# The down product of two feed-forward networks by Strassen's scheme, with sums on VectorE and GpSimd

## The chip, the core and the metric

The kernel runs on one NeuronCore of a Trainium2 chip. Its engines are TensorE (PE, matrix products; its weight loads are shown as PEld), VectorE (DVE), ScalarE (ACT), GpSimd (POOL) and SyncE (SP, which issues most DMAs here). Each engine executes its own instructions strictly in the order in which the program lists them; between engines, semaphores make one wait for another. Matrix products accumulate in PSUM, everything else works on tiles in SBUF, and DMAs move data between DRAM and SBUF. The metric is the time on the device of one launch, in microseconds (us). Three runs of the kernel before took 3050.97 to 3052.87 us, median 3051.56.

## The reference

The model is one layer of a hybrid decoder over 16 meta tokens and 1024 tokens, with 1024 features: a half-step SwiGLU network, a middle part (chunked gated DeltaNet beside RWKV-7, merged and projected), a second half-step SwiGLU network, and a final RMS norm. The meta tokens are dropped from the output. The change touches the two networks, each of which adds half of this to the hidden state:

```python
def _swiglu(x, w_gu, w_down):
    gate, up = jnp.split(x @ w_gu, 2, axis=-1)
    return (jax.nn.silu(gate) * up) @ w_down
```

`w_gu` has 1024 x 5632 elements, `w_down` 2816 x 1024. All inputs are float32.

## The kernel before

Features lie on the 128 partitions and tokens run along a row, so a row block is 128 features by all tokens: 8 row blocks for the hidden state `h` (in the second network `hh`), 22 for the 2816 hidden features. The first network (`ffn1`, L647) has 1040 tokens, the second (`ffn2`, L729) 1024.

A float32 product is made of three TensorE products: each operand is split into a high and a low part (`split`, L155: ScalarE copies the high part, VectorE subtracts to get the low one), and high x high, high x low and low x high are summed in PSUM.

Weights come through `fetchw` (L216). In the order of a generator, it loads a raw tile `wraw` (two buffers) on SyncE's queue and splits it into a tile `w` (two buffers). `loadw` takes the next tile and has the one after it fetched. A raw buffer is free again when VectorE has read it, and a `w` buffer when TensorE has used it.

`gate_up` (L435) makes the two input products by a scheme of Strassen's kind, with 7 products instead of 8 of half blocks; in it GpSimd makes sums of weights (L418 to L421). It multiplies gate and up on VectorE (L538) and stores each hidden row block half by half to the DRAM tensor `hid` (`store`, L477). `Hidden` (L561) loads those rows again, whole, into `hr` (three buffers, 520 or 512 KB each) and splits them into `hd`. The first three loads are issued before `gate_up` ends.

`down` (L606) is the plain product. The 22 hidden rows come in groups of 6, 6, 5 and 5 (`GROUPS`). For each group and each of 8 output blocks m there is one weight tile, 768 or 640 columns wide, that serves two token chunks (528 + 512 tokens in the first network, 512 + 512 in the second; `halves` cuts 528 into 256 and 272). A product `pd` of a group and a chunk accumulates in PSUM, and VectorE adds half of it to `h` (L624). In the last group the chunks run one after the other, so that its weight tiles are loaded twice, and after each block a hook does the norm that follows: in `ffn1` the sums of squares and the scaled input of the middle part, in `ffn2` the final norm and the output. `h` is loaded again for this stage, on GpSimd's queue (L687, L770). `Rms` (L265) squares on ScalarE, adds on VectorE (L281), and sums over the partitions by a TensorE product with ones (L292).

The whole order of each engine is fixed when the program is built.

## Time and profile before

The profile is of one execution, whose span, from its first to its last instruction, is 3046.4 us; the median of the runs is 5.2 us longer, for what lies around the span.

| what | value |
|---|---|
| runs | 3050.97, 3051.56, 3052.87 us |
| span of the profiled execution | 3046.4 us |
| TensorE, VectorE, ScalarE, GpSimd busy | 97%, 66%, 45%, 11% of the span |
| mean granted clock of TensorE | 0.993 |
| matmuls of `down` (`pd`) | 2448 + 192, from 473.3 to 3031.1 us |
| weight tiles of `down` loaded | 48 of 320 KB, 32 of 384 KB |
| hidden loads `hr` | 22 of 520 KB, 22 of 512 KB |

"Busy" counts an instruction from its start to its end; matmuls overlap, so the duration of one matmul is not the time it takes up in a sequence. A row of a timeline gives the start, the duration, the engine, the line, the operation, what it writes and reads, and in brackets how long the engine was idle before and which instruction it waited for. A row of windows gives, for a stretch, each engine's busy time with its number of instructions, then the granted clock, the mean busy share of the 16 DMA engines and the GB/s that they moved.

### The profile page before, as it was taken

How to read it: one execution, taken by the hardware profiler on the slowest of the kernel's cores; microseconds unless marked ns; L12 is line 12 of the kernel's file. 1: busy time of each engine (PE TensorE's matmuls, PEld its weight loads, DVE VectorE, ACT ScalarE, POOL GpSimd, SP SyncE). 2: the span in 40 equal slices, each digit the busy share in tenths (PEclk: the TensorE clock that was granted, in tenths of full speed). 3: DMA queues.
4: the chain of work that ended last, by engine and by line, in shares of the span. 5: the costliest groups of instructions: out<-in, count | busy, mean ns of one | idle time of the engine just before them, and what ended most of it. 6: DMA issues, size and time to landing. Idle time of an engine off the chain costs nothing.

```text
span 3046.4 us, 61663 instructions
## 1 busy us (share of the span) xinstructions
PE 2942.3 (97%) x25498; PEld 2530.1 (83%) x25498; DVE 2007.7 (66%) x3872; ACT 1372.2 (45%) x2404; POOL 348.6 (11%) x503
## 2 busy tenths in 40 slices
PE   8999999999989999999998999999999999999998
PEld 8999998998878888888776777777786888888886
DVE  7555554346668877778868888777766755556246
ACT  5322222125645656556565655665544432223114
POOL 0322220000000000000000110010000032232000
PEclk9999999999999999999999999999999999999999
DMA  3232224234222322233332333223345132225223
GB/s 127 83 98 84 83 82 160 81 94 149 80 67 72 78 74 67 78 82 97 82 92 67 91 80 81 74 74 88 106 145 178 64 104 90 83 83 202 58 80 115
DMA packets 257593, 287.19 MB, mean 94 GB/s; under 512 B 169296, under 2 KB 175440, under 8 KB 257312
## 3 DMA queue, kind: packets, MB, share of 16 engines
q1 hardware_dynamic: 253072, 271.43, 30.2%
q0 software_dynamic: 2512, 8.65, 0.8%
q8 instruction: 201, 3.29, 0.5%
q10 hardware_dynamic: 1728, 3.16, 0.3%
q14 instruction: 80, 0.66, 0.1%
HBM read 232.70 MB, written 50.47 MB: 93 GB/s over the span
## 4 chain that ended last, share of the span: by engine, by line
PE 52%; DVE 10%; ACT 5%; issue 2%; DMA 1%; SPq 0%; DVEq 0%; ACTq 0%
PE pp L261 16%; PE pg L448 13%; PE pd L261 8%; PE pwo L261 3%; PE pg L472 1%; DVE w L160 1%; DVE tb L1400 1%; DVE Xb L1402 1%; ACT w L159 1%; PE vp L1085 1%; PE cs L1032 1%; PE mp L1085 1%; PE np L1085 1%; DVE mt L1508 1%; PE bkt L1317 1%
## 5 line engine op out<-in xcount | busy, mean ns | idle before, releaser
L261 PE MATMUL pp<-uk,w 128*128 128x512 f32 (+2 forms) x4824 | 966.6, 346 | 9.3 <-DVE w L160 5.7
L261 PEld LDWEIGHTS pp<-uk,w 128*128 128x128 f32 x4824 | 741.3, 190 | 105.5 <-DVE w L160 13.2
L159 ACT ACTIVATE w<-wraw 128x1024 fp32r<-128x1024 f32 (+2 forms) x330 | 326.4, 989 | 497.5 <-PE pd L261 301.7
L261 PE MATMUL pd<-hd,w 128*128 128x512 f32 (+2 forms) x2448 | 454.4, 346 | 5.3 <-ACT hd L159 3.1
L160 DVE TENSOR_TENSOR w<-wraw,w 128x1024 fp32r<-128x1024 f32 (+2 forms) x330 | 403.2, 1222 | 74.8 <-ACT w L159 64.9
L261 PEld LDWEIGHTS pd<-hd,w 128*128 128x128 f32 x2448 | 391.8, 189 | 63.9 <-ACT hd L159 3.3
L448 PE MATMUL pg<-bt,w 128*128 128x256 f32 (+2 forms) x2520 | 400.7, 317 | 0.0
L448 PEld LDWEIGHTS pg<-bt,w 128*128 128x128 f32 x2520 | 360.4, 188 | 32.8
L454 DVE TENSOR_TENSOR c<-c,pg 128x520 f32<-128x520 f32 (+1 forms) x280 | 189.6, 689 | 278.3 <-PE pg L448 250.6
L448 PE MATMUL pg<-b,w 128*128 128x256 f32 (+2 forms) x2160 | 347.8, 317 | 0.0
L448 PEld LDWEIGHTS pg<-b,w 128*128 128x128 f32 x2160 | 309.8, 188 | 28.0
L159 ACT ACTIVATE w<-wrx 128x1024 fp32r<-128x1024 f32 (+1 forms) x64 | 58.4, 913 | 289.8 <-PE pg L448 247.9
L418 POOL TENSOR_TENSOR wrx<-wrx 128x512 f32<-128x512 f32 x38 | 52.5, 1382 | 732.8 <-DVE w22b L160 519.0
L1402 DVE TENSOR_TENSOR Xb<-Xb,tb 115x126 f32<-115x126 f32 (+22 forms) x496 | 125.4, 253 | 9.1 <-DVE tb L1400 0.4
L1400 DVE TENSOR_TENSOR tb<-Ub,Xb 115x126 f32<-115x126 f32 (+22 forms) x496 | 124.1, 250 | 8.1 <-DMA Ub<-scr 0.9
L1209 DVE SCALAR_TENSOR_TENSOR acc<-xr,pk,acc 128x528 f32<-128x528 f32 (+1 forms) x144 | 108.8, 756 | 28.6 <-ACT acc L1205 28.0
L624 DVE SCALAR_TENSOR_TENSOR h<-pd,h 128x528 f32<-128x528 f32 (+1 forms) x64 | 44.6, 698 | 116.4 <-PE pd L261 116.4
L624 DVE SCALAR_TENSOR_TENSOR hh<-pd,hh 128x512 f32<-128x512 f32 x64 | 44.1, 690 | 115.2 <-PE pd L261 115.2
L261 PE MATMUL pwo<-uk,w 128*128 128x512 f32 x384 | 99.7, 413 | 4.1 <-DVE w L160 1.9
L261 PEld LDWEIGHTS pwo<-uk,w 128*128 128x128 f32 x384 | 73.8, 197 | 21.9 <-ACT w L159 2.7
L160 DVE TENSOR_TENSOR w<-wrx,w 128x1024 fp32r<-128x1024 f32 (+1 forms) x64 | 66.6, 1041 | 14.9 <-ACT w L159 14.8
L159 ACT ACTIVATE hd<-hr 128x1040 fp32r<-128x1040 f32 (+1 forms) x40 | 41.2, 1061 | 63.3 <-DMA hr<-hid 38.3
(420 smaller groups left out, 4200.4 us busy)
## 6 DMA issues: line engine op xcount, KB each, us to landing
wraw<-in_win SPq DMA_DIRECT2D x150, 512.0 KB
wraw<-in_wgu SPq DMA_DIRECT2D x44, 512.0 KB
wrx<-in_wgu SPq DMA_DIRECT2D x44, 512.0 KB
wraw<-in_wdn SPq DMA_DIRECT2D x48, 320.0 KB
wraw<-in_wdn SPq DMA_DIRECT2D x32, 384.0 KB
hid<-c SPq DMA_DIRECT2D x44, 260.0 KB
hr<-hid SPq DMA_DIRECT2D x22, 520.0 KB
hid<-c SPq DMA_DIRECT2D x44, 256.0 KB
```

The costliest lines, as they stand in the source:

```text
L159: g.nc.scalar.activation(hi, src, AF.Copy)
L160: (eng or g.nc.vector).tensor_tensor(lo, src, hi.bitcast(F32), op=ALU.subtract)
L261: g.nc.tensor.matmul(ps, lhsT=l, rhs=r, start=i == 0, stop=i == n - 1)
L418: sums.tensor_tensor(a22, a21, a22, op=ALU.add)
L448: nc.tensor.matmul(ps[:, c0 : c0 + cn], lhsT=l[:, x, k, :], rhs=r[:, k, y, c0 : c0 + cn], start=i == 0, stop=i == 3 * HK - 1)
L454: nc.vector.tensor_tensor(o, x, y, op=ALU.add)
L472: nc.tensor.matmul(ps[:, c0 : c0 + cn], lhsT=l[:, x, k, :], rhs=r[:, k, y, c0 : c0 + cn], start=i == 0, stop=i == 6 * HK - 1)
L624: nc.vector.scalar_tensor_tensor(hv, pd, 0.5, hv, op0=ALU.mult, op1=ALU.add)
L1085: g.nc.tensor.matmul(ps[e][HS[dst], c0 : c0 + CB], lhsT=l, rhs=r, start=True, stop=True)
L1209: nc.vector.scalar_tensor_tensor(acc[:, :n], xr[:, tap : tap + n], V("convw", ct * 4 + tap), acc[:, :n], op0=ALU.mult, op1=ALU.add)
L1400: nc.vector.tensor_tensor(tv, U[:, i, i + 1 :].unsqueeze(2).to_broadcast([npt, nt, ncc]), X[:, i, 0:ncc].unsqueeze(1).to_broadcast([npt, n ...
L1402: nc.vector.tensor_tensor(X[:, i + 1 :, 0:ncc], X[:, i + 1 :, 0:ncc], tv, op=ALU.add)
```

## The change

The product becomes one of 2 x 2 blocks: output rows 0 to 511 and 512 to 1023, hidden rows 0 to 1407 and 1408 to 2815, and two halves of the tokens (520 or 512 each). Winograd's form of Strassen's scheme needs 7 products of half blocks where the plain product has 8. For each of them the hidden side is a *form*, in the order `b11`, `t1`, `t2`, `b22`, `t3`, `b21`, `t4`: three blocks of the hidden rows and four differences. `gate_up` makes the differences with four more subtractions on VectorE for each pair of row blocks, and stores 7 x 11 rows of one half's width to `frm`.

The weight side is a block as it is (forms 0, 5, 6) or a sum or difference of blocks (forms 1 to 4), made by GpSimd in a resident tile `wsum`, each from the one before and one raw tile; forms 1 and 4 also load a second block straight into `wsum`. `down` then runs rounds over the forms and, in each, over four output blocks m with two weight tiles, of 6 and 5 row blocks of hidden features. Each product is added, halved, to up to four blocks of `h` (`ADDS`: 4, 2, 3, 1, 2, 1, 1). Hidden tiles have 28 slots and three buffers `hr` of half the former size.

In the first network the last two rounds run twice, first for columns 256 to 519, then for 0 to 255 (`by_columns`), so that the norm after them begins before all is done; the second sum of squares there is added by GpSimd. In the second network the final norm of one half of the tokens is made after round 4, that of the other at the end.

```diff
+CHUNKS = ((0, 6), (6, 5))
+
+FORMS = ("b11", "t1", "t2", "b22", "t3", "b21", "t4")
+ADDS = ((0, 1, 2, 3), (1, 3), (1, 2, 3), (1,), (2, 3), (0,), (2,))
+NSLOT = 28
+LAST = len(FORMS) - 2
...
+def down_rounds(by_columns):
+
+    for r in range(LAST):
+        yield r, None
+    for cols in ((256, T // 2 - 256), (0, 256)) if by_columns else (None,):
+        for r in range(LAST, len(FORMS)):
+            yield r, cols
...
-        f = 0
-        for G in GROUPS:
-            for _ in range(2 if f + G == NF else 1):
-                for m in range(KD):
-                    yield f"wdn{n}", (m, slice(None), slice(f, f + G)), G
-            f += G
+        for r, _ in down_rounds(n == 1):
+            for m in range(HK):
+                for k0, kk in CHUNKS:
+                    yield f"wdn{n}", (r, m, k0), kk
...
+def down_weights(g, name, raw, r, m, k0, kk):
+
+    blk = lambda i, j: g.a[name][m + HK * i][:, HF * j + k0 : HF * j + k0 + kk]
+    dma = g.nc.sync.dma_start
+    sums = g.nc.gpsimd.tensor_tensor
+    dma(raw, blk(*((0, 0), (1, 1), (0, 0), (0, 1), (1, 0), (0, 1), (1, 1))[r]))
+    if r in (0, LAST, LAST + 1):
+        return raw
+    s = g.wsum[:, m, k0 : k0 + kk]
+    if r == 1:
+        dma(s, blk(1, 0))
+        sums(s, s, raw, op=ALU.add)
+    elif r == 2:
+        sums(s, s, raw, op=ALU.subtract)
+    elif r == 3:
+        sums(s, raw, s, op=ALU.subtract)
+    else:
+        dma(s, blk(0, 0))
+        sums(s, s, raw, op=ALU.subtract)
+    return s
...
-    raw = g.wp.tile([P, KD, P], F32, name="wraw", tag="wraw", bufs=2)
-    g.nc.sync.dma_start(raw[:, :kk, :], g.a[name][idx])
+    raw = g.wp.tile([P, KD, P], F32, name="wraw", tag="wraw", bufs=2)[:, :kk]
+    if name.startswith("wdn"):
+        src = down_weights(g, name, raw, *idx, kk)
+    else:
+        src = raw
+        g.nc.sync.dma_start(raw, g.a[name][idx])
     w = g.wp.tile([P, 2, KD, P], F32R, name="w", tag="w", bufs=WB)
-    split(g, raw[:, :kk, :], w[:, 0, :kk, :], w[:, 1, :kk, :])
+    split(g, src, w[:, 0, :kk, :], w[:, 1, :kk, :])
...
+    def sub(o, x, y, p, form):
+        nc.vector.tensor_tensor(o, x, y, op=ALU.subtract)
+        store(o, p, form)
...
+            mul(c12, g12, p)
+            sub(g11, c12, c11, p, "t1")
+            sub(g22, c22, g11, p, "t2")
+            sub(c12, c22, c12, p, "t3")
...
+            mul(c21, g21, p, "b21")
+            sub(g21, c21, g22, p, "t4")
...
+    def fill(self, upto):
+        while len(self.at) < min(upto, len(self.order)):
+            rp = self.order[len(self.at)]
+            if not self.raws:
+                self.load()
+            t = self.slots.pop(0)
+            split(self.g, self.raws.pop(0), t[:, 0, :], t[:, 1, :])
+            self.at[rp] = t
...
-def down(g, sp, hs, which, chunks, hooks, hidden, bufs):
+def down(g, hs, which, n, hidden, hooks):
...
-    f0 = 0
-    for G in GROUPS:
-        hid = hidden.tiles(sp, f0, G, bufs)
-        last = f0 + G == NF
-        if last:
-            hooks.before_last()
-        for ci, cs in enumerate([[c] for c in chunks] if last else [chunks]):
-            for m in range(KD):
-                wd = loadw(g, f"wdn{which}", m, slice(None), slice(f0, f0 + G))
-                for t0, n in cs:
-                    pd = mm_tile(g, "pd", n)
-                    for c0, cn in halves(n):
-                        sl = slice(t0 + c0, t0 + c0 + cn)
-                        mm3(g, pd[:, c0 : c0 + cn], wd, G, lambda k: (hid[k][:, 0, sl], hid[k][:, 1, sl]))
-                    hv = hs[m][:, t0 : t0 + n]
-                    nc.vector.scalar_tensor_tensor(hv, pd, 0.5, hv, op0=ALU.mult, op1=ALU.add)
-                if last:
-                    hooks.after_block(ci, m)
-        f0 += G
+    hidden.fill(HF + 5)
+    for r, cols in down_rounds(which == 1):
+        hidden.fill(HF * (r + 1))
+        for m in range(HK):
+            pd = mm_tile(g, "pd", n)
+            parts = [cols] if cols else halves(n)
+            for k0, kk in CHUNKS:
+                wd = loadw(g, f"wdn{which}", r, m, k0)
+                for c0, cn in parts:
+                    for k in range(k0, k0 + kk):
+                        x = hidden.at[r, k]
+                        for i, (u, v) in enumerate(((0, 0), (0, 1), (1, 0))):
+                            nc.tensor.matmul(pd[:, c0 : c0 + cn], lhsT=wd[:, u, k - k0, :], rhs=x[:, v, c0 : c0 + cn],
+                                             start=k + i == 0, stop=k == HF - 1 and i == 2)
+            c0, cn = cols or (0, n)
+            for o in ADDS[r]:
+                t0 = o % 2 * n + c0
+                hv = hs[m + o // 2 * HK][:, t0 : t0 + cn]
+                nc.vector.scalar_tensor_tensor(hv, pd[:, c0 : c0 + cn], 0.5, hv, op0=ALU.mult, op1=ALU.add)
+            hooks.after(r, cols, m)
+            if r <= LAST:
+                hidden.fill(HF * r + 16 + 3 * (m + 1))
...
+        pairs = [k + i * HK for k in range(HK) for i in range(2)]
+        for k in pairs:
             nc.gpsimd.dma_start(hs[k], g.a["hT"][k])
+        sum_tile = lambda shape, dtype: sp.tile(shape, dtype, name="wsum", tag="wsum", bufs=1)
+        g.wsum = sum_tile([P, HK, HF, P], F32)
+        keep = [slot_tile(sp, n, f"fa{i}") for i in range(17)]
+        early = ExitStack()
+        ep = early.enter_context(tc.tile_pool(name="f1e", bufs=1, reuse_waits="tile"))
+        ring = keep[2:] + [slot_tile(ep, n, f"fb{i}") for i in range(NSLOT - 17)] + keep[:2]
+        hidden.slots = (2 * ring)[: LAST * HF] + keep[1:]
...
-            hooks.rms = [Rms(g, lambda: g.un.tile([P, 528], F32, name="nsq", tag="nsq", bufs=4), n)
-                         for _, n, _ in SEGS]
+            hooks.rms = [Rms(g, lambda: g.un.tile([P, 528], F32, name="nsq", tag="nsq", bufs=4), n,
+                             add_on=nc.gpsimd if s else None) for s, (_, n, _) in enumerate(SEGS)]
...
+            if r < LAST:
+                if r == LAST - 1 and m == HK - 1:
+                    before_last()
+                return
+            s = 0 if cols[0] else 1
...
+        def final_tiles(s):
+            new = lambda tag, m: sp.tile([P, m, n], F32, name="fin", tag=tag, bufs=1)
+            ts = [new("wsum", 11)] if s else [new(f"fs{i}", 2) for i in unused]
+            rows = [t[:, i, :] for t in ts for i in range(t.shape[1])]
+            hooks.rs, hooks.rows = rows[3], rows[4:]
+            it = iter(range(100))
+            return Rms(g, lambda: rows[next(it) % 3], n)
+
+        def after(r, cols, m):
+            s, k = int(r < LAST), m + HK * (r - LAST)
+            blk = lambda k: hs[k][:, s * n : (s + 1) * n]
+            if k < 0 and k + 1:
+                return
+            if s or k == 0:
+                hooks.sum = final_tiles(s)
+            for i in range(KD - 1) if s else [k] * (k < KD - 1):
+                hooks.sum.add(blk(i))
+            if not s and k < KD - 1:
+                return
+            rs = hooks.rs
+            hooks.sum.finish(rs, blk(KD - 1))
```

On VectorE, where the first network passes from `gate_up` to `down`. The rows of before: `hd` are splits of hidden rows, `w` splits of weight tiles, `h` the sums; the last row of `gate_up` stands first.

```order
L538 TENSOR_TENSOR c21_4826<-c21_4826,c21_4677 128x520
L160 TENSOR_TENSOR hd_4970<-hr_4639,hd_4970 128x1040
L160 TENSOR_TENSOR hd_4973<-hr_4641,hd_4973 128x1040
L160 TENSOR_TENSOR hd_4978<-hr_4976,hd_4978 128x1040
L160 TENSOR_TENSOR hd_4983<-hr_4981,hd_4983 128x1040
L160 TENSOR_TENSOR hd_4988<-hr_4986,hd_4988 128x1040
L160 TENSOR_TENSOR hd_5492<-hr_5490,hd_5492 128x1040
L624 SCALAR_TENSOR_TENSOR h0_4953<-pd_4991,h0_4953 128x528
L624 SCALAR_TENSOR_TENSOR h0_4953<-pd_5029,h0_4953 128x512
L160 TENSOR_TENSOR w_5051<-wraw_5049,w_5051 128x768
```

The same place of the change, from the fourth hidden split on (`fa` are slots for hidden tiles):

```order
L165 TENSOR_TENSOR fa5_5052<-hr_5084,fa5_5052 128x520
L165 TENSOR_TENSOR fa6_5053<-hr_5088,fa6_5053 128x520
L165 TENSOR_TENSOR fa7_5054<-hr_5092,fa7_5054 128x520
L165 TENSOR_TENSOR fa8_5055<-hr_5096,fa8_5055 128x520
L165 TENSOR_TENSOR fa9_5056<-hr_5100,fa9_5056 128x520
L165 TENSOR_TENSOR w_5175<-wraw_5173,w_5175 128x768
L165 TENSOR_TENSOR fa10_5057<-hr_5104,fa10_5057 128x520
L165 TENSOR_TENSOR fa11_5058<-hr_5108,fa11_5058 128x520
L165 TENSOR_TENSOR fa12_5059<-hr_5112,fa12_5059 128x520
L165 TENSOR_TENSOR fa13_5060<-hr_5116,fa13_5060 128x520
L673 SCALAR_TENSOR_TENSOR h0_5033<-pd_5136,h0_5033 128x520
L673 SCALAR_TENSOR_TENSOR h0_5033<-pd_5136,h0_5033 128x520
```

Where six whole hidden rows were split ahead of the first sum, there are twelve halves and a weight tile now, and more hidden splits follow between the sums.

On VectorE in the middle of a group before (only sums and weight tiles):

```order
L160 TENSOR_TENSOR w_5240<-wraw_5238,w_5240 128x768
L624 SCALAR_TENSOR_TENSOR h4_4957<-pd_5243,h4_4957 128x528
L624 SCALAR_TENSOR_TENSOR h4_4957<-pd_5281,h4_4957 128x512
L160 TENSOR_TENSOR w_5303<-wraw_5301,w_5303 128x768
L624 SCALAR_TENSOR_TENSOR h5_4958<-pd_5306,h5_4958 128x528
```

In round 1 of the change, for one output block m; behind it GpSimd's sums of the same round:

```order
L165 TENSOR_TENSOR w_5644<-wsum_5046,w_5644 128x768
L165 TENSOR_TENSOR fa8_5055<-hr_5778,fa8_5055 128x520
L165 TENSOR_TENSOR fa9_5056<-hr_5782,fa9_5056 128x520
L165 TENSOR_TENSOR fa10_5057<-hr_5868,fa10_5057 128x520
L673 SCALAR_TENSOR_TENSOR h1_5035<-pd_5596,h1_5035 128x520
L673 SCALAR_TENSOR_TENSOR h5_5036<-pd_5596,h5_5036 128x520
L165 TENSOR_TENSOR w_5696<-wsum_5046,w_5696 128x640
L165 TENSOR_TENSOR fa11_5058<-hr_5872,fa11_5058 128x520
L165 TENSOR_TENSOR fa12_5059<-hr_5876,fa12_5059 128x520
```

```order
L239 TENSOR_TENSOR wsum_5046<-wsum_5046,wraw_5549 128x768
L239 TENSOR_TENSOR wsum_5046<-wsum_5046,wraw_5597 128x640
L239 TENSOR_TENSOR wsum_5046<-wsum_5046,wraw_5640 128x768
L239 TENSOR_TENSOR wsum_5046<-wsum_5046,wraw_5692 128x640
L239 TENSOR_TENSOR wsum_5046<-wsum_5046,wraw_5735 128x768
```

Each step has two weight splits that read `wsum`, with two or three hidden splits of the next round among them, and GpSimd has two sums for it, where it had none in this stage.

On TensorE before, in the first group of the first network, where one weight tile passes from the first chunk to the second:

```order
L261 MATMUL pd_5306<-hd_4983,w_5240 128x272 x3
L261 MATMUL pd_5306<-hd_4988,w_5240 128x272 x3
L261 MATMUL pd_5344<-hd0_4823,w_5240 128x512 x3
L261 MATMUL pd_5344<-hd_4970,w_5240 128x512 x3
L261 MATMUL pd_5344<-hd_4973,w_5240 128x512 x3
```

And in a round by columns of the change:

```order
L667 MATMUL pd_7005<-fa5_5052,w_6944 128x264 x3
L667 MATMUL pd_7005<-fa6_5053,w_6944 128x264 x3
L667 MATMUL pd_7005<-fa7_5054,w_7008 128x264 x3
L667 MATMUL pd_7005<-fa8_5055,w_7008 128x264 x3
L667 MATMUL pd_7005<-fa9_5056,w_7008 128x264 x3
L667 MATMUL pd_7005<-fa10_5057,w_7008 128x264 x3
L667 MATMUL pd_7005<-fa11_5058,w_7008 128x264 x3
L667 MATMUL pd_7061<-fa1_5048,w_7031 128x264 x3
```

A weight tile that served 54 matmuls of two chunks (18 each of 256, 272 and 512 columns) serves 15 or 18 of 264 columns here.

165 lines of the change are left out of this document (79 added, 86 removed).

## The prediction

> **What bounds the kernel now.** I read the page first: the busy line of each engine, and the shares of the chain that ended last.
>
> ```profile
> span 3046.4 us, 61663 instructions
> PE 2942.3 (97%) x25498; PEld 2530.1 (83%) x25498; DVE 2007.7 (66%) x3872; ACT 1372.2 (45%) x2404; POOL 348.6 (11%) x503
> ...
> PE 52%; DVE 10%; ACT 5%; issue 2%; DMA 1%; SPq 0%; DVEq 0%; ACTq 0%
> PE pp L261 16%; PE pg L448 13%; PE pd L261 8%; PE pwo L261 3%; PE pg L472 1%; DVE w L160 1%; DVE tb L1400 1%; DVE Xb L1402 1%; ACT w L159 1%; PE vp L1085 1%; PE cs L1032 1%; PE mp L1085 1%; PE np L1085 1%; DVE mt L1508 1%; PE bkt L1317 1%
> ```
>
> TensorE is the bound over the whole span. The shares are averages, so next come windows over the stages that change: both `down` stages, the tail, the crowded starts, two calm stretches, and one in which GpSimd makes weight sums.
>
> ```profile
> core 0: us, PE busy (x) PEld busy (x) DVE busy (x) ACT busy (x) POOL busy (x), PEclk, DMA share, GB/s
> 473.40:731.50 258.10, 253.72 (x1588) 230.11 (x1587) 120.48 (x153) 63.83 (x83) 9.56 (x18) 0.99 0.39 125
> 2788.70:3031.60 242.90, 241.96 (x1061) 198.80 (x1061) 109.68 (x139) 61.00 (x77) 10.58 (x17) 1.00 0.35 110
> 3031.60:3046.40 14.80, 1.92 (x4) 0.30 (x2) 6.81 (x7) 5.12 (x6) 2.93 (x2) 0.73 0.38 142
> 480.00:494.00 14.00, 10.48 (x64) 9.61 (x63) 5.03 (x5) 4.78 (x5) 1.67 (x4) 0.88 1.01 410
> 2794.00:2811.00 17.00, 17.00 (x77) 14.08 (x76) 8.70 (x10) 5.34 (x6) 5.99 (x12) 1.00 1.03 400
> ...
> 2850.00:2900.00 50.00, 50.00 (x222) 41.44 (x221) 15.88 (x20) 6.03 (x7) 0.00 (x0) 1.00 0.21 59
> 100.00:150.00 50.00, 50.00 (x421) 50.00 (x420) 27.39 (x33) 14.26 (x19) 17.09 (x12) 1.00 0.27 86
> ```
>
> Both stages are matmul all the way (253.7 of 258.1 us, 242.0 of 242.9), at a granted clock of 0.99 and 1.00. The side engines have room: VectorE 15.9 of 50 us. Matmuls removed shorten the span, until a side engine has less than a step's work of cover. DMA is full (1.01, 1.03) while each stage starts. The stages' matmuls, and the two-input sums:
>
> ```profile
> L261 PE MATMUL pd<-hd,w x2448: 274/389/799, 473.3 to 3031.1; 128*128 128x512 f32 x106, 128*128 128x272 f32 x43, 128*128 128x256 f32 x40
> ...
> L261 PE MATMUL pd<-hdb,w x192: 389/389/390, 2789.2 to 2852.9; 128*128 128x512 f32 x192
> L624 DVE SCALAR_TENSOR_TENSOR h<-pd,h x64: 680/697/709, 490.8 to 732.2; 128x528 f32<-128x528 f32 x32, 128x512 f32<-128x512 f32 x32
> ```
>
> **What it removes.** A matmul's own duration (389 ns) overlaps its neighbour's; what counts is the step between evictions in matmul-bound code. In `gate_up` one product is 24 matmuls 256 or 264 wide in the first network, 12 of 512 in the second; in the first `down` a 528-wide product is 30 matmuls.
>
> ```profile
> 462.00 0.69 DVE L454 TENSOR_TENSOR c<-c,pg 128x520 f32<-128x520 f32 x1 [2.17 <-PE pg L448]
> 464.86 0.70 DVE L454 TENSOR_TENSOR c<-c,pg 128x520 f32<-128x520 f32 x1 [2.17 <-PE pg L448]
> ```
> ```profile
> 2777.84 0.69 DVE L454 TENSOR_TENSOR c<-c,pg 128x512 f32<-128x512 f32 x1 [2.03 <-PE pg L448]
> 2780.56 0.69 DVE L454 TENSOR_TENSOR c<-c,pg 128x512 f32<-128x512 f32 x1 [2.03 <-PE pg L448]
> ```
> ```profile
> 699.99 0.71 DVE L624 SCALAR_TENSOR_TENSOR h<-pd,h 128x528 f32<-128x528 f32 x1 [1.40 <-PE pd L261]
> ...
> 703.68 0.71 DVE L624 SCALAR_TENSOR_TENSOR h<-pd,h 128x528 f32<-128x528 f32 x1 [1.42 <-PE pd L261]
> ...
> 708.12 0.69 DVE L624 SCALAR_TENSOR_TENSOR h<-pd,h 128x512 f32<-128x512 f32 x1 [2.18 <-PE pd L261]
> ...
> 732.24 0.68 DVE L624 SCALAR_TENSOR_TENSOR h<-pd,h 128x512 f32<-128x512 f32 x1
> ```
>
> That is 2.86/24 = 0.1194 us, 2.72/12 = 0.2267 us, and 3.69/30 = 0.123 us. From 708.12 to 732.24 there are seven products of 15 matmuls 512 wide, so 0.230 each. Before, the first `down` had 8 blocks x 22 rows x 3 = 528 triples of 256, 272 and 512 columns: 528 x (0.246 + 0.230) = 251.2 us, so 6.9 of its 258.1 us are loss. Now: 7 forms x 4 x 11 x 3 x 2 = 1848 at 0.1194 = 220.7. The second had 1056 x 0.2267 = 239.4 (loss 3.5); now 924 = 209.5. **The gross gain is 30.5 + 29.9 = 60.4 us**, an eighth of each. What follows takes some of it back.
>
> **Extra work in `gate_up`.** 44 subtractions more per network, 0.69 us each, 30 us over a stage of 400 us in which VectorE works 27.4 of 50 us even beside GpSimd's sums. It rises to about 31 of 50. I take 0 (up to 4 if one holds up an eviction).
>
> **Round 0 of each network.** Work that was spread over four groups of hidden rows comes early. In FFN1's round 0, TensorE needs 4 x 66 x 0.1194 = 31.5 us. VectorE has about 25 hidden splits at half of a 1040-wide one (0.69 with overhead), 8 weight splits (0.96 and 0.83) and 16 adds at 0.70: 35.6 us. DMA carries 25 x 0.266 = 6.7 MB of hidden rows, about 2 MB of late h, some 5 MB of weights with the first of the resident sums, 1.3 MB of stores: 15 MB, at the 0.41 MB/us that the full window shows 37 us. Before, that crowding cost one wait of 3.1 us and smaller ones; TensorE was busy for 52.2 of the first 56.6 us:
>
> ```profile
> 473.40:530.00 56.60, 52.23 (x318) 46.40 (x317) 23.06 (x26) 9.49 (x10) 3.67 (x7) 0.97 0.55 197
> ```
> ```profile
> PE pd L261 <- ACT hd L159: 3.1, 1, 3.1
> PE pd L261 <- DVE hd L160: 1.2, 2, 0.7
> ```
>
> I take a loss of 10 us in FFN1 (7 to 14) against 4.4 before, and 5.5 in FFN2 (3 to 9), whose start had no stall.
>
> The Trainium skill ("DMA: Bandwidth & Descriptors", section "Where 436 GB/s comes from") says that transfers between HBM and SBUF are held to about 358 GB/s by HBM. The trace disagrees: 410 and 400 GB/s in the two windows. By the page, FFN1's round 0 would take 42 us and cost 5 us more; the measurement decides.
>
> **Rounds 1 to 4: weight sums on GpSimd.** 16 steps per network, each with one 768-wide and one 640-wide sum. The only rows are 512-wide, from `gate_up`:
>
> ```profile
> L418 POOL TENSOR_TENSOR wrx<-wrx x38: 1278/1288/1691, 92.0 to 2758.7; 128x512 f32<-128x512 f32 x38
> ```
> ```profile
> 204.78 0.70 DVE L538 TENSOR_TENSOR c<-c,c 128x520 f32<-128x520 f32 x1
> 205.40 2.31 DVE L160 TENSOR_TENSOR w<-wraw,w 128x1024 fp32r<-128x1024 f32 x1
> ```
> ```profile
> 204.89 1.74 POOL L421 TENSOR_TENSOR wraw<-wraw 128x512 f32<-128x512 f32 x1
> ```
>
> By size 1.29 becomes 1.93 and 1.61: 3.54 us a step. Beside VectorE operations with two SBUF inputs the durations grow: the sum begun at 204.89 took 1.74, and the split begun at 205.40 took 2.31 and ended 1.1 us after the sum did. A split of that width takes 1.22 when nothing runs beside it:
>
> ```profile
> 729.89 1.22 DVE L160 TENSOR_TENSOR w<-wraw,w 128x1024 fp32r<-128x1024 f32 x1
> ```
>
> So they seem to take turns. VectorE's two-input splits in a step are 2.75 hidden (1.9) and two of weights (1.8), 3.7 us. With the sums that is 7.24 us of a step of 33 x 0.2267 = 7.48 (FFN2) or 66 x 0.1194 = 7.88 (FFN1). The adds read PSUM and one SBUF operand. If they too take turns, the steps of rounds 1 to 4 need 8.62, 9.31, 7.93 and 8.62 us, and the excess is 18.2 us in FFN2 and 11.8 in FFN1. If all of it hides, 0. I take 6 and 4, nearer to hiding: in 100 to 150 us GpSimd was busy for 17.1 of 50 us and TensorE never waited.
>
> The Trainium skill ("SBUF — State Buffer", section "Who interferes with whom") says that a VectorE instruction with two SBUF inputs and a GpSimd instruction that reads SBUF exclude each other, and that one with a single SBUF input does not contend. The rows above agree with the first half. By it 7.24 us a step are serial; without it 3.7 beside 3.54. It speaks against this change, and is behind the third case below.
>
> **FFN1's last rounds by columns.** Rounds 5 and 6 run twice, half the columns at a time: 16 steps, each with two fresh weight tiles for only 33 matmuls, 33 x 0.1194 = 3.94 us. A raw weight buffer (two of them) is loaded, copied by ScalarE, subtracted by VectorE, and loaded again. The trace shows that circle in FFN2, in the order ScalarE, VectorE, SyncE, and then DMA traffic until it ends:
>
> ```profile
> 2829.52 0.85 ACT L159 ACTIVATE w<-wraw 128x768 fp32r<-128x768 f32 x1 [7.31 <-PE pd L261]
> ```
> ```profile
> 2830.40 0.96 DVE L160 TENSOR_TENSOR w<-wraw,w 128x768 fp32r<-128x768 f32 x1 [0.19 <-ACT w L159]
> 2831.39 0.33 SPq L222 DMA_DIRECT2D wraw<-in_wdn  x1
> ```
> ```profile
> 2833.50:2834.00 0.50, 0.50 (x4) 0.42 (x3) 0.40 (x1) 0.00 (x0) 0.00 (x0) 1.00 0.77 307
> 2834.00:2834.50 0.50, 0.50 (x4) 0.42 (x3) 0.29 (x1) 0.00 (x0) 0.00 (x0) 1.00 0.00 0
> ```
>
> The load lands 2.65 us after VectorE's end; with 0.85, 0.96 and hand-overs the circle is 4.7 us, and about 4.9 with the second buffer's load and the norm's work beside it. That exceeds 3.94: (4.9 - 3.94) x 16 = **16 us** (10 to 26). Before, each tile fed at least 15 matmuls of 512 (3.45 us, two in 6.9), so the circle hid.
>
> **Hand-overs.** FFN1's second sum of squares moves to GpSimd (1.29 for 0.69 at the very end, then the norm waits): 1.3. FFN2 puts the norm of its first half into one lump ahead of a weight split: 1.5 (0 to 4). The tail after the last add keeps its 14.8 us.
>
> **The sum.** FFN1: 220.7 + 10 + 4 + 16 + 1.3 + 2.5 (what was lost before outside the start) = 254.5 for 258.1, so -3.6. FFN2: 209.5 + 5.5 + 6 + 1.5 + 3.5 (as before) = 226.0 for 242.9, so -16.9. The span becomes 3046.4 - 20.5 = 3025.9. The runs' median of 3051.56 is 5.2 above the span, so **3031 us**.
>
> **The rivals.**
> - *Side engines hide nearly everything*: round 0 no worse than before, sums free, the circle at 4.7. Then -60.4 + 12 + 1.3 = -47, 3004 us. For it: VectorE is idle for two thirds of the calm windows. Against: 35.6 and 37 us of work in 31.5.
> - *Sums and VectorE fully in turn*: 18.2 + 11.8 for my 10, so 20 more, 3051 us, no change. For it: the split at 205.40. Against: the calm 100 to 150.
> - *Slower: weights land late in the column rounds.* With two raw buffers the step is the landing time plus 2.05 us and hand-overs. From 4.6 us landing (a step of 6.6) the loss eats the gain and the kernel is slower by over 0.2%. The nearest row of a landing under traffic is 5.5 us:
>
> ```profile
> hh<-h2dr POOLq DMA_DIRECT2D x8, 256.0 KB, 5.5
> ```
>
>  Then a step is 7.55, 42 us more than my sum: 3073 us. Against: no hidden loads are left in those rounds, only stores of h.
> - *The matmul count does not fall*: 3050 us and more. The order shows 1848 + 924 of them, so hardly possible.
>
> **How the numbers follow.** Forecast 3019 to 3043: 0.52. Hidden: 0.17. In turn: 0.19. Late weights: 0.1. No fewer matmuls: 0.02. Range 3004 to 3056, which leaves out most of the late weights and the far side of hiding. Within 0.2% (6 us, about what a measurement of this kernel can tell): most of the third case, 0.15; slower 0.13; faster 0.72.
>
> **What would show it.** Evictions of L673 2.72/12 x 33 = 7.48 us apart in FFN2's rounds 5 and 6, and 7.9 in FFN1's rounds 1 to 4, are the gain; 4.9 us apart in the column rounds is the circle. Round 0 should show waits for hidden splits. GpSimd's sums of 1.9 and 1.6 us, stretched beside splits, show the turns. I am wrong if rounds 1 to 4 take over 8.6 us a step, or if the column steps stay at 3.94.

## The result, and the profile after

The changed kernel takes 3103.61 us (median of 4 runs, 3100.70 to 3106.87) where the kernel before, run beside it, takes 3051.65. The ratio is 1.0162, with a 95% interval from 1.0148 to 1.0177: 52 us **slower**. The prediction was 3031 us, with a range up to 3056.

The page of the profiled execution, the rows that answer to those of before:

```profile
span 3105.1 us, 63103 instructions
PE 2928.2 (94%) x25630; PEld 2519.8 (81%) x25630; DVE 2192.1 (71%) x4103; ACT 1456.7 (47%) x2562; POOL 493.1 (16%) x574
...
PE 66%; DVE 15%; DMA 8%; ACT 7%; issue 3%; SPq 0%; POOL 0%; DVEq 0%; ACTq 0%; POOLq 0%
```

The span is 59 us longer than before, while the medians of the runs differ by 52: the profiled execution is the slowest of the four runs. In these runs the time is 1.8 to 3.3 us above the span, so a part of the 5.2 us that the prediction added to the span is a difference between runs and not time around the span.

TensorE is busy for only 14 us less than before, although 60 us of matmuls are gone, because the matmuls that are left ran more slowly in places (mean granted clock 0.981, before 0.993). Its idle time rose by 73 us, more than the matmuls had taken. In the chain that ended last, DMA rose from 1% to 8%.

The windows of the stages (columns as in the windows before: length, busy time of each engine with its instructions, granted clock, DMA share, GB/s). In order: round 0, rounds 1 to 4 and the rounds by columns of the first network; the end of the second network's `gate_up`; its round 0, rounds 1 to 4, rounds 5 and 6:

```profile
474.40:531.80 57.40, 40.89 (x271) 37.95 (x270) 35.34 (x53) 20.97 (x33) 5.10 (x5) 0.82 0.82 278
531.80:679.00 147.20, 133.27 (x1057) 130.60 (x1057) 102.19 (x115) 52.67 (x80) 56.63 (x30) 0.97 0.60 183
679.00:770.00 91.00, 76.16 (x530) 68.75 (x528) 53.34 (x75) 39.51 (x59) 8.85 (x6) 0.96 0.62 171
2811.80:2843.00 31.20, 23.82 (x92) 18.69 (x91) 15.30 (x24) 6.13 (x9) 3.75 (x8) 0.84 0.48 156
2843.20:2885.90 42.70, 35.19 (x136) 27.21 (x135) 29.49 (x43) 15.97 (x25) 9.22 (x11) 0.92 0.89 297
2885.90:3022.60 136.70, 126.62 (x529) 100.18 (x528) 105.40 (x119) 58.00 (x90) 57.50 (x30) 0.98 0.64 203
3022.60:3090.30 67.70, 63.49 (x267) 50.69 (x267) 31.56 (x41) 23.34 (x32) 2.96 (x2) 0.97 0.34 104
```

No stage is matmul all the way any more, and no side engine is busy all the way either (VectorE 102 of 147 us). So TensorE waits for chains across several engines, and the table of what it waits for in the first `down` shows for which:

```profile
PE pd L667 <- DVE w L165: 23.4, 27, 3.6
PE pd L667 <- ACT w L164: 10.6, 14, 1.8
PE pd L667 <- ACT fa L164: 6.7, 1, 6.7
PE pd L667 <- DVE fa L165: 3.6, 3, 3.3
PE nps L330 <- POOL nsq L319: 1.9, 1, 1.9
PE pp L299 <- ACT w L164: 1.4, 1, 1.4
```

Each row says who waits for whom, the us in total, how often, and the longest. 34 us are for weight splits, in 41 waits of at most 3.6; 10 us are for hidden splits, nearly all in two long waits.

The waits do not hold all of it. After a long one the matmuls themselves are slow. TensorE's timeline at the start of round 0, and then windows of 7 us at the same place:

```profile
477.96 2.08 PE L667 MATMUL pd<-fa,w 128*128 128x256 f32 x8 [3.31 <-DVE fa L165]
486.77 0.58 PE L667 MATMUL pd<-fa,w 128*128 128x256 f32 x1 [6.73 <-ACT fa L164]
```
```profile
480.00:487.00 7.00, 0.27 (x2) 0.23 (x1) 0.25 (x1) 0.64 (x1) 1.06 (x2) 0.50 1.01 361
487.00:494.00 7.00, 6.70 (x27) 5.84 (x28) 1.85 (x4) 1.97 (x4) 0.00 (x0) 0.50 1.04 409
496.00:503.00 7.00, 6.92 (x57) 6.72 (x57) 2.65 (x5) 2.28 (x4) 0.00 (x0) 1.00 0.96 327
```

With the granted clock at 0.50, 27 matmuls take 6.7 us; at 1.00, 57 take 6.9. The wait of 6.7 us costs some 3.5 us more after it has ended.

What stood in the way at that place is on SyncE's queue. The hidden loads `hr` of round 0 share it with the loads of second blocks into `wsum`, which only round 1 needs:

```profile
480.48 0.82 SPq L238 DMA_DIRECT2D wsum<-in_wdn  x2
481.34 1.39 SPq L623 DMA_DIRECT2D hr<-frm  x3
482.77 0.90 SPq L238 DMA_DIRECT2D wsum<-in_wdn  x2
487.48 2.47 SPq L623 DMA_DIRECT2D hr<-frm  x3
490.00 0.92 SPq L238 DMA_DIRECT2D wsum<-in_wdn  x2
```

The second network lost time before its `down` had begun, at 2843 us. Its h is loaded on GpSimd's queue in 16 loads. The slots of four of its rows are free earlier than before, and eight loads start between 2811 and 2815 us, the first and the last of them below. Then ScalarE, which splits hidden rows ahead of time, waits 8 us for a hidden load, and the split of a `gate_up` weight tile is queued behind that instruction:

```profile
2811.26 0.56 POOL L834 DMA_DIRECT2D hh<-h2dr  x1
...
2814.98 0.57 POOL L834 DMA_DIRECT2D hh<-h3dr  x1
```
```profile
2820.17 0.63 ACT L164 ACTIVATE hdb<-hr 128x512 fp32r<-128x512 f32 x1 [8.02 <-DMA hr<-frm]
2822.03 0.63 ACT L164 ACTIVATE hdb<-hr 128x512 fp32r<-128x512 f32 x1 [1.23 <-DMA hr<-frm]
2822.57 1.04 ACT L164 ACTIVATE w<-wrx 128x1024 fp32r<-128x1024 f32 x1
```
```profile
2825.65 1.22 PE L486 MATMUL pg<-bt,w 128*128 128x512 f32 x2 [6.75 <-ACT w L164]
```

In rounds 1 to 4, VectorE and GpSimd at one place:

```profile
2904.95 4.30 DVE L165 TENSOR_TENSOR hdb<-hr,hdb 128x512 fp32r<-128x512 f32 x2
```
```profile
2904.58 4.12 POOL L241 TENSOR_TENSOR wsum<-wsum,wraw 128x768 f32<-128x768 f32 x2 [2.04 <-DMA wraw<-in_wdn]
```

Two hidden splits, 0.69 us each when alone, take 4.30 us while two sums run: they end when the sums have ended (2909.25 and 2908.70).

In the rounds by columns, one raw weight buffer once around, on SyncE, ScalarE and VectorE:

```profile
701.01 0.33 SPq L233 DMA_DIRECT2D wraw<-in_wdn  x1
701.43 0.38 SPq L773 DMA_DIRECT2D hdr<-h  x1
```
```profile
704.79 0.84 ACT L164 ACTIVATE w<-wraw 128x768 fp32r<-128x768 f32 x1 [2.15 <-DMA wraw<-in_wdn]
```
```profile
705.66 0.96 DVE L165 TENSOR_TENSOR w<-wraw,w 128x768 fp32r<-128x768 f32 x1 [2.17 <-ACT w L164]
```

From the load's issue to the next one's, after VectorE's end at 706.62, are 5.6 us, and so far apart are the sums of these rounds. From the load's issue to the start of the ScalarE copy that waits for it are 3.78 us, with a store of h issued right behind the load; that the store is what made it longer was not tested.

### The profile page after: what moved, and what is told of

The parts are those of the page before. It is cut to its first block, busy times and chain, and to the rows that moved or that the text cites. A ratio compares the mean times of both kernels' runs of the same rounds, so it can differ in the third digit from the quotient of the medians.

```text
span 3105.1 us, 63103 instructions
## 1 busy us (share of the span) xinstructions
PE 2928.2 (94%) x25630; PEld 2519.8 (81%) x25630; DVE 2192.1 (71%) x4103; ACT 1456.7 (47%) x2562; POOL 493.1 (16%) x574
## 4 chain that ended last, share of the span: by engine, by line
PE 66%; DVE 15%; DMA 8%; ACT 7%; issue 3%; SPq 0%; POOL 0%; DVEq 0%; ACTq 0%; POOLq 0%
PE pg L486 24%; PE pp L299 18%; PE pd L667 5%; DMA hr<-frm 4%; DVE w L165 3%; PE pg L510 3%; PE pwo L299 3%; ACT w L164 2%; DMA wraw<-in_wdn 2%; DVE tb L1482 1%; DVE Xb L1484 1%; PE vp L1167 1%; PE cs L1114 1%; PE mp L1167 1%; PE bkt L1399 1%
## 5 line engine op out<-in xcount | busy, mean ns | idle before, releaser
L165 DVE TENSOR_TENSOR w<-wraw,w 128x1024 fp32r<-128x1024 f32 (+2 forms) x314 | 393.8, 1255 | 112.4 <-ACT w L164 105.2
L164 ACT ACTIVATE w<-wraw 128x1024 fp32r<-128x1024 f32 (+2 forms) x314 | 314.4, 1002 | 284.6 <-PE pg L486 130.4
L667 PE MATMUL pd<-fa,w 128*128 128x256 f32 (+1 forms) x1200 | 173.5, 299 | 40.5 <-DVE w L165 19.1
L667 PEld LDWEIGHTS pd<-fa,w 128*128 128x128 f32 x1200 | 159.7, 201 | 51.1 <-DVE w L165 24.7
L667 PE MATMUL pd<-fs,w 128*128 128x512 f32 x636 | 155.8, 401 | 14.0 <-ACT w L164 7.6
L667 PEld LDWEIGHTS pd<-fs,w 128*128 128x128 f32 x636 | 122.0, 194 | 45.4 <-ACT w L164 9.8
L165 DVE TENSOR_TENSOR w<-wsum,w 128x768 fp32r<-128x768 f32 x64 | 75.0, 1173 | 24.5 <-ACT w L164 24.1
L164 ACT ACTIVATE w<-wsum 128x768 fp32r<-128x768 f32 x64 | 50.2, 785 | 83.5 <-PE pd L667 67.0
```

The costliest lines, as they stand in the source:

```text
L164: g.nc.scalar.activation(hi, src, AF.Copy)
L165: (eng or g.nc.vector).tensor_tensor(lo, src, hi.bitcast(F32), op=ALU.subtract)
L667: nc.tensor.matmul(pd[:, c0 : c0 + cn], lhsT=wd[:, u, k - k0, :], rhs=x[:, v, c0 : c0 + cn], start=k + i == 0, stop=k == HF - 1 and i == 2)
```

## The experiments

Stages are read off the timelines: a round ends with VectorE's first sum of its last output block, and the last stage of each network with its last `pd` matmul. "Matmuls alone" is the count by the cadence of the prediction. "Between" is from the first network's last `pd` matmul to the second network's first; the figure in the first row is that of the kernel before. The total is the median of all runs of that kernel, and between runs of one kernel it differs by up to 17 us, much more than for the kernel before.

Only one profiled execution of each kernel has stages, so a difference of a stage counts only where it is larger than what the stage shows without a reason. Rounds 5 and 6, for example, took 63.7 to 68.6 us in kernels that are alike there. "Between" varies most: the part of it up to the second `gate_up`, which hardly any of the edits touches, took 1634 to 1644 us (before the change 1632).

| kernel | total us (runs) | net 1: round 0 | 1-4 | columns | between | net 2: round 0 | 1-4 | 5-6 |
|---|---|---|---|---|---|---|---|---|
| matmuls alone | | 31.5 | 126.1 | 63.0 | 2057.0 | 29.9 | 119.7 | 59.9 |
| the change | 3103.6 (4) | 57.4 | 147.2 | 90.5 | 2073.7 | 42.7 | 136.7 | 67.3 |
| e1 h on SyncE | 3100.5 (2) | 55.8 | 149.8 | 89.6 | 2061.8 | 37.7 | 143.7 | 67.1 |
| e2 second blocks late | 3083.6 (2) | 53.0 | 137.2 | 90.4 | 2068.4 | 39.3 | 136.7 | 68.6 |
| e3 no sums, no second blocks | 3051.8 (8) | 51.5 | 127.6 | 89.4 | 2072.1 | 38.5 | 120.4 | 67.0 |
| e4 third raw buffer | 3082.6 (2) | 56.0 | 147.1 | 73.0 | 2072.7 | 42.1 | 138.3 | 68.2 |
| f1 sums aside | 3089.5 (1) | 56.5 | 143.1 | 89.5 | 2065.0 | 41.0 | 137.2 | 63.7 |
| f2 second blocks, no sums | 3060.4 (1) | 57.0 | 126.5 | 89.6 | 2068.2 | 38.0 | 123.6 | 67.0 |
| f4 sums on VectorE | 3073.8 (2) | 55.2 | 131.8 | 89.5 | 2072.2 | 39.3 | 127.6 | 67.9 |
| f3 = e1 + e2 + e4 | 3063.6 (4) | 52.5 | 137.5 | 70.7 | 2065.8 | 36.9 | 141.1 | 68.1 |
| f5 = f3 + f4 | 3052.8 (8) | 50.9 | 130.6 | 72.5 | 2068.9 | 37.4 | 128.5 | 67.2 |
| g2 = f5, h and ck late | 3044.5 (8) | 47.9 | 135.2 | 71.3 | 2073.0 | 36.7 | 133.2 | 68.5 |
| g3 = g2, norm spread | 3042.5 (8) | 48.1 | 132.8 | 74.0 | 2070.3 | 36.7 | 129.6 | 64.9 |
| g5 = g3, few hidden loads | 3027.3 (1) | 39.6 | 133.4 | 70.9 | 2067.3 | 38.3 | 124.4 | 63.3 |
| h1 = g3, two waits | 3040.1 (6) | 50.6 | 130.1 | 72.3 | 2068.2 | 36.9 | 130.7 | 63.2 |

**e1: h of the second network on SyncE's queue.** The rows of h are put into a list and issued four at a time, behind the hidden loads 8, 12, 16 and 20 (`issue_after` puts an instruction behind another on its engine):

```diff
-                    nc.gpsimd.dma_start(hs[m][:, s * n : (s + 1) * n], g.h3dr[m] if s else g.h2dr[m])
+                    hidden.later.append((hs[m][:, s * n : (s + 1) * n], g.h3dr[m] if s else g.h2dr[m]))
```

> The second network's h is loaded on SyncE's queue, four rows at a time behind the hidden loads 8, 12, 16 and 20, and no longer on GpSimd's queue at 2811 us. Theory (early loads of h push back the hidden loads, and a weight split queued behind a hidden split on ScalarE waits with them): the wait of 6.75 us in gate_up and the slow matmuls behind it go, 3104 becomes 3091 to 3096. Rival (the hidden loads collide with each other): the wait stays above 4 us, 3101 to 3106.

The wait of 6.75 us is gone. At the same place there are now two short ones, of 0.44 us and this:

```profile
2816.86 8.01 PE L486 MATMUL pg<-bt,w 128*128 128x512 f32 x34 [1.12 <-DVE w L165]
```

The stretch between the networks shrank by 11.9 us. Of these, 8.7 are at the end of `gate_up`: its last 92 matmuls up to the second `down` took 31.7 us in the change and 23.0 here (20.9 before). The other 3 us lie in the middle part, which the edit does not touch. Round 0 shrank by 5.0, and rounds 1 to 4 got 7.0 us longer. The two runs are 3095.9 and 3105.1 us, so the total does not show the gain.

What follows is that the early loads of h cause the wait. Their size is less sure: the six other kernels that keep these loads where the change has them wait 1.8 to 4.1 us there and take 25.8 to 28.6 us for the 92 matmuls, and those with this edit 21.4 to 24.7.

**e2: second blocks late.** 

```diff
-        dma(s, blk(1, 0))
+        with g.tc.issue_after(g.hrload.ins):
+            dma(s, blk(1, 0))
```

(and the same for `blk(0, 0)`; `g.hrload` is the last hidden load that the program has issued.)

> The loads of second weight blocks into the resident sum tile are queued on SyncE behind the hidden loads that stand before them in the program. Theory (eight of them, 2.9 MB, go ahead of the hidden loads of round 0): round 0 of the first network shrinks from 57 us to 42 to 48, that of the second from 43 to 36 to 40, total 3082 to 3092. Rival (hidden loads, h and stores fill DMA anyway, so only the order of the same bytes changes): round 0 stays above 53 us, total 3098 or more.

The total fell by 20 us, inside the expectation, but not where it was expected: round 0 of the first network became only 4.4 us shorter, and its rounds 1 to 4 became 10 us shorter. The second blocks are a part of round 0's trouble, not its main part.

**e3: no sums.** Forms 1 to 4 return the raw tile at once in `down_weights`; all weight sums and second blocks are left out.

```diff
-    if r in (0, LAST, LAST + 1):
-        return raw
+    return raw
```

> Leaves out all 64 weight sums and the loads of second blocks: forms 1 to 4 use one raw block. Theory (sums on GpSimd and two-input operations of VectorE take turns, and the sum stands in the weight chain): rounds 1 to 4 fall from 148 to about 130 us in the first network and from 137 to about 123 in the second, and round 0 falls too; total 3045 to 3060. Rival (in rounds 1 to 4 SyncE's queue, with hidden loads ahead of weight loads, is what makes weights late): rounds 1 to 4 stay above 140 and 131 us, total 3075 or more.

Rounds 1 to 4 fell to 127.6 and 120.4 us, within 1.5 us of their matmuls. Without the sums and the second blocks, neither the hidden loads nor SyncE's queue holds TensorE up in these rounds: the rival falls.

**e4: a third raw buffer in the rounds by columns.** One more buffer of 768 columns, used for every third tile; two norm buffers less make the room.

```diff
-    raw = g.wp.tile([P, KD, P], F32, name="wraw", tag="wraw", bufs=2)[:, :kk]
+    if name == "wdn1" and idx[0] >= LAST and hasattr(g, "un") and g.wfetched % 3 == 0:
+        raw = g.un.tile([P, 6, P], F32, name="wrd", tag="wrd", bufs=1)[:, :kk]
+    else:
+        raw = g.wp.tile([P, KD, P], F32, name="wraw", tag="wraw", bufs=2)[:, :kk]
```

> The rounds by columns have a third raw weight buffer (one norm buffer less of each kind to make room). Theory (the circle of a raw buffer sets the step, 5.6 us): the step falls to 4.2 to 4.6 us, 16 to 22 us less, total 3082 to 3088. Rival (the DMA or ScalarE's and VectorE's work sets it): step above 5.2 us, total 3097 or more.

VectorE's sums in these rounds, in that run:

```profile
688.69 0.43 DVE L676 SCALAR_TENSOR_TENSOR h<-pd,h 128x264 f32<-128x264 f32 x1
692.94 0.43 DVE L676 SCALAR_TENSOR_TENSOR h<-pd,h 128x264 f32<-128x264 f32 x1
697.15 0.43 DVE L676 SCALAR_TENSOR_TENSOR h<-pd,h 128x264 f32<-128x264 f32 x1
```

These steps are 4.2 us now, not 5.6, and the rounds take 17.5 us less: the circle of the raw buffer set the step.

**f1, f2, f4: which part of the sums.** Three edits of `down_weights`, each on the changed kernel alone. f1 makes every sum, but the split reads the raw tile (so the sums don't reach the product):

```diff
-    return s
+    return raw
```

> GpSimd makes all its sums, but the weight splits read the raw block instead of the sum (so the sums are left out of the product). Theory A (taking turns on VectorE's and GpSimd's two-input operations is what rounds 1 to 4 lose): they stay at 140 us or more in the first network and 130 or more in the second. Theory B (the sum is one more link between a weight's landing and its split): they fall to 132 and 125 or less.

f2 leaves the sums out and keeps the loads of second blocks:

```diff
-    if r == 1:
-        dma(s, blk(1, 0))
-        sums(s, s, raw, op=ALU.add)
...
-    return s
+    if r in (1, 4):
+        dma(s, blk(1, 0) if r == 1 else blk(0, 0))
+    return raw
```

> The sums are left out, the loads of second blocks stay where they were. Against the run without both, only those loads come back: theory (the loads cost round 0 and the start of round 1, not the rest): round 0 of the first network 55 to 58 us as in the change, rounds 1 to 4 within 4 us of 127 and 120. Rival (the loads also hold up rounds 1 to 4): over 134 or over 127.

f4 makes the sums on VectorE:

```diff
-    sums = g.nc.gpsimd.tensor_tensor
+    sums = g.nc.vector.tensor_tensor
```

> The same sums on VectorE instead of GpSimd. If taking turns is the loss, VectorE has 1.8 us more a step but GpSimd's 3.5 us are gone: rounds 1 to 4 fall to 130 to 138 and 121 to 130 us, total 3078 to 3092. If the sum's place in the chain, or VectorE's own load, is the loss, they stay above 142 and 132, total 3098 or more.

With the sums aside, rounds 1 to 4 stay at 143 and 137 us although no weight split reads a sum: the place ahead of the split is not it. With the loads alone they are 126.5 and 123.6. With the same sums on VectorE, which then has 1.8 us more to do a step, they fall by 15.4 and 9.1 us, and the total by 30.

VectorE's own time shows why moving the sums away from it gave nothing. In rounds 1 to 4 of the first network it is busy for 102.2 us with the sums on GpSimd, and for 101.7 us when it makes them itself. Its splits of hidden rows, in the change and then in f4 (number of instructions, us in total, mean ns of one, idle time before them):

```profile
L165 DVE TENSOR_TENSOR fa<-hr,fa 128x520 fp32r<-128x520 f32 x33 | 33.0, 1029 | 14.9 <-ACT fa L164 14.9
```
```profile
L165 DVE TENSOR_TENSOR fa<-hr,fa 128x520 fp32r<-128x520 f32 x32 | 21.7, 694 | 6.8 <-ACT fa L164 6.5
```

A split takes 1.03 us on average beside GpSimd's sums and 0.69 without them. The waits of TensorE in rounds 1 to 4 of the second network, first in the change (2886 to 3022 us), then with VectorE's sums (2880 to 3010):

```profile
PE pd L667 <- DVE w L165: 7.8, 7, 2.1
PE pd L667 <- ACT w L164: 2.2, 3, 0.9
```
```profile
PE pd L667 <- ACT w L164: 3.1, 2, 2.4
PE pd L667 <- DVE w L165: 2.6, 3, 1.5
```

The waits for VectorE's splits fall to a third. So having the sums on GpSimd costs 15.4 of the 21.1 us that these rounds lose in the first network and 9.1 of 17.0 in the second, and it lengthens VectorE's splits. How much comes by the longer splits alone is not separated. A raw weight tile can be loaded again only when its sum is made, and SyncE's loads of raw tiles in these rounds of the first network waited 48.9 us for GpSimd's sums, 32.8 for VectorE's in f4. f1 keeps such waits: there the loads of second blocks waited 20.6 us for the sums.

**f3 and f5: the edits together.** f3 has e1, e2 and e4; f5 has f4 too.

> The three edits together: h of the second network on SyncE's queue, second blocks loaded late, a third raw buffer in the rounds by columns. If their gains are separate (12 us ahead of the second down stage, about 15 around rounds 0 and 1, 17 in the rounds by columns), the total is 3056 to 3066; if they share one cause, 3072 or more.

> The three edits of the run before and the sums on VectorE. If taking turns is what rounds 1 to 4 still lose, they fall from 137.5 and 141 to 128 to 133 and 124 to 129 us, and the total is 3036 to 3048: the change no longer costs anything against the kernel before. If VectorE becomes the bound with the other edits in, rounds 1 to 4 stay above 136 and the total above 3053.

f3 is 3063.6 us, within the expectation: 40 us less than the change, where the three edits alone gave 3, 20 and 21. With VectorE's sums it is 3052.8, somewhat above what was expected (its ratio to the kernel before is 1.0009, 0.9997 to 1.0020): rounds 1 to 4 came to 130.6 and 128.5, as expected. So far an eighth of `down`'s matmuls is gone for nothing.

**g2, g3: three more places.** g2 queues three rows of the first network's h and the load of the 600 KB input `ck` behind hidden loads, with the same two devices as e1 and e2. g3 spreads the final norm of the second network's first half over rounds 5 and 6:

```diff
-            for i in range(KD - 1) if s else [k] * (k < KD - 1):
-                hooks.sum.add(blk(i))
+            if k < HK:
+                for i in range(2 * k, min(2 * k + 2, KD - 1)):
+                    sum1.add(blk(1, i))
...
+            elif k < KD - 1:
+                for i in range(3 * (k - HK), min(3 * (k - HK) + 3, KD)):
+                    out(1, i, rs1, rows1)
```

> As the last, and in the first network the three rows of h that are loaded at the start of round 0 and the 600 KB of ck are queued behind hidden loads. Theory (they stand in DMA ahead of the fourth to twelfth hidden row): the wait of 4.5 us and its slow matmuls shrink, round 0 falls from 52.5 to 43 to 49 us, total 4 to 9 below the last. Rival (the hidden loads cannot begin before gate_up ends and so are late in any case): round 0 stays above 50 us.

> As the last, and the final norm of the first finished half in the second network is spread over rounds 5 and 6, two squares or three outputs an output block, instead of one lump after round 4. Theory (the lump puts five outputs ahead of a weight split on VectorE): rounds 5 and 6 fall from 68 to 60 to 63 us, total 5 to 8 below the last. Rival (spread, the same work holds up every step a little): above 66 us.

g2 gained 8 us in total and 3 in round 0, which at 47.9 is inside its expectation; its profiled execution (span 3054.4) lies at the upper end of its runs (3042.0 to 3056.3), so its stages don't add up to its median. Its ratio to the kernel before is 0.9982 (0.9971 to 0.9994). g3 took rounds 5 and 6 from 68.5 to 64.9, less than expected, and its total is 3042.5 us: ratio 0.9971 (0.9960 to 0.9982), 0.3% faster than the kernel before. The intervals of g2 and g3 overlap, and f1, without g3's edit, has 63.7 us in rounds 5 and 6, so what the spreading is worth is not settled.

**g5 and h1: what keeps round 0, and two last waits.** In g5, eight of round 0's eleven hidden rows are not loaded, in both networks; their slots are split from the third row's raw tile, so those rows are missing from form 0, and VectorE's work is the same. h1 queues the second blocks behind a hidden load six earlier, and takes the last square of the first network straight into the product with ones:

```diff
+            if not (s and k == KD - 1):
+                rms.add(hs[k][:, t0 : t0 + sn])
...
-                rms.finish(rs)
+                rms.finish(rs, hs[k][:, t0 : t0 + sn] if s else None)
```

> As the run with the norm spread, but in round 0 of both networks eight of the eleven hidden rows are not loaded: their slots are split from the third row's raw tile (so these rows of form 0 are left out of the product). Theory (round 0 waits for hidden rows that cannot be loaded before gate_up's buffers are free): round 0 falls from 48 to 36 to 40 us in the first network and from 37 to 30 to 33 in the second. Rival (VectorE's order of splits and adds, 35 us of work, is the bound): above 43 and above 34.

> As the run with the norm spread, with two edits: the second blocks are queued behind a hidden load six earlier (round 1 of the second network waited 5.6 us for the first of them), and the last square of the first network's second sum goes straight into the product with ones, without GpSimd's last add (3.1 us of waiting there). If both waits are what they look like, 5 to 9 us less: 3034 to 3038. If the loads then collide with round 0's hidden loads again, no gain: 3041 or more.

TensorE's waits in g5, from 470 to 510 us:

```profile
476.46 23.37 PE L686 MATMUL pd<-fa,w 128*128 128x256 f32 x169 [3.31 <-DVE fa L165]
500.52 13.33 PE L686 MATMUL pd<-fa,w 128*128 128x256 f32 x106 [0.70 <-ACT w L164]
```

Where g3 has eight waits up to 510 us, two are left. Round 0 of the first network falls to 39.6 us: there, the eight hidden loads, their lateness and their traffic together, are worth 8.5 of the 16.6 us that were left (one run), and the wait of 3.31 us ahead of the first split is not among them. In the second network round 0 did not fall (38.3), as the rival has it; TensorE's one long wait there is 4.7 us for a weight split on ScalarE, and what holds the round up is not settled.

h1 comes to 3040.1 us, ratio 0.9960 (0.9945 to 0.9974). This is the lowest median of a complete version, but its interval overlaps that of g3. The wait of 3.1 us at the first network's end became 1.3, and that of 5.6 us in round 1 became 3.5, while round 0 of the first network took 50.6 us instead of 48.1, so the total lies between the two expectations.

## Why the prediction was wrong

**The gross gain was right.** In rounds 5 and 6 of the second network, where little else goes on, the sums of two output blocks are 33 x 0.2267 = 7.48 us apart, as predicted:

```profile
3060.41 0.69 DVE L673 SCALAR_TENSOR_TENSOR hh<-pd,hh 128x512 f32<-128x512 f32 x1 [1.51 <-PE pd L667]
3067.89 0.69 DVE L673 SCALAR_TENSOR_TENSOR hh<-pd,hh 128x512 f32<-128x512 f32 x1 [1.51 <-PE pd L667]
```

And e3's rounds 1 to 4 stand within 1.5 us of the matmul count. The 60.4 us were there; against them stood 129.5 us of losses in the profiled execution (58.7 of longer span, the 60.4, and the 10.4 that the stages had lost before), where the prediction had 50. Term by term, loss over the matmuls alone:

| term | predicted | measured | shown by |
|---|---|---|---|
| round 0, first network | 10 | 25.9 | e2, g2, g5 |
| rounds 1 to 4, first | 4 | 21.1 | e3, f1, f2, f4 |
| by columns | 16 | 27.5 | e4 |
| end of `gate_up`, second | 0 | 10.8 | e1 |
| round 0, second | 5.5 | 12.8 | e1, in part |
| rounds 1 to 4, second | 6 | 17.0 | e3, f1, f4 |
| rounds 5 and 6, second (norm in one lump) | 1.5 | 7.4 | not settled (g3) |

**The step that failed most is the choice in rounds 1 to 4**: "I take 6 and 4, nearer to hiding". The mechanism was on record, with the row at 205.40, as the case "in turn"; the choice went against it because in 100 to 150 us GpSimd worked and TensorE never waited. But there GpSimd's 17 us in 50 met 27 of VectorE; in these rounds 57 us in 147 meet 102, mostly two-input splits. A step took 9.2 us in the first network and 8.5 in the second, where the prediction named 8.6 as the sign of being wrong. The first network's 21 us lie even beyond the bound of 11.8, which counted only VectorE's operations in turn. TensorE's waits there are 13.9 us, and its busy time is 7.2 us above the count, at a granted clock of 0.97. With VectorE's sums (f4) these two are 3.6 and 2.0. The Trainium skill ("SBUF — State Buffer", section "Who interferes with whom") has the rule that a VectorE instruction with two SBUF inputs and a GpSimd instruction that reads SBUF exclude each other; the split times above, 1.03 us beside the sums and 0.69 without, agree with it.

**Round 0** was mis-sized: the bytes were about right (278 GB/s over 57.4 us are 16 MB, predicted 15), but the rate of 0.41 MB/us was reached only in stretches (409 GB/s from 487 to 494 us), and the sum took DMA as one bucket to be emptied in time. What counted besides was the order in it: which hidden row lands first. The hidden loads themselves were worth 8.5 us (g5); what stood ahead of them 4.4 (e2) and 3.0 (g2, against f5). In g5, 8.1 us are left; 4 of them are two waits.

**The rounds by columns** had the right mechanism and a wrong size: a landing of 2.65 us, taken at a place without such stores, was 3.78 here, beside the stores of h. That makes 5.6 us a step instead of 4.9. It did not reach the 4.6 us from which the rival on late weights would have decided alone.

**`gate_up` was taken to cost nothing.** The prediction counted its subtractions, which did hide. It missed that half of the second network's h, in other slots now, is loaded from 32 us ahead of the start of `down` (before, one of the 16 loads was 23 us ahead, and the others began 2 us behind the start) and met the hidden loads, and that a weight split stands behind a hidden split on ScalarE. The windows show it. At this place TensorE was busy for all of 31.5 us before, as the row below has it; now it is busy for 23.8 of 31.2.

```profile
2757.00:2788.50 31.50, 31.50 (x140) 26.10 (x139) 21.85 (x25) 10.86 (x13) 7.42 (x5) 1.00 0.50 154
```

**The rivals.** None of the four on record is what happened. The kernel became slower because the terms came out beyond their upper ends, or close to it, all together, where the sum took each near its middle and the slower case hung on one mechanism alone. The terms of the table are 122.5 of the 129.5 us. Another 5.5 lie between the first `down` and the second `gate_up`; the hand-over has waits of 1.4 and 1.9 us of these (predicted: 1.3 in all), and where the rest comes from was not traced.

## What to carry to other kernels

When matmuls are taken out of a stage that is matmul all the way, price the chain that then ends last by its slowest link under traffic, and look at what the freed buffers let start early, on every queue. Putting two-input elementwise work on an idle GpSimd instead of VectorE did not pay here: VectorE was no less busy, and 30 us came back when it did the sums itself. And a wait is dearer than its length where it is long enough to lower the granted clock.

## What was not expected of the hardware

A wait of 6.7 us (twice: at 480 and 2819 us) was followed by 7 to 8 us at a granted clock of 0.50, in which, at the first place, a matmul of 256 columns took 0.25 us instead of 0.12. A wait of 3.3 us was enough for that too: in g5, TensorE had 0.50 for the 5 us behind it (476.4 to 481.4 us), and 1.00 from 482.4 on. The prediction priced no wait with this. The Trainium skill ("TensorE: Matmul & The Clock Gate", section "What's actually happening") says that the clock falls to half after an idle window of about 3.4 us and is whole again after about as long a busy one; the first half agrees roughly with these rows, and the slow stretches here, 5 to 8 us, were longer.

Times of the changed kernels spread more between runs than those of the kernel before (f3: 3056.5 to 3073.9; before, beside it: 3046.1 to 3050.5). No run here shows why.
